# The first MLP product of the first layer by seven products of half blocks for eight, its operands in large tiles

## The chip, the cores and the metric

The kernel runs on one core of one Trainium2 chip. The metric is the device time of one execution in microseconds; the time of the kernel before is the median of three runs. The engines are PE (TensorE, the matmuls), DVE (VectorE), ACT (ScalarE), POOL (GpSimd) and SP (SyncE, which here issues the transfers). Each takes its instructions strictly in the order in which they stand in its program.

## The reference, cut to what matters

A trunk of two layers on 512 latent tokens and 256 context tokens of width 1024. Each layer has an attention part and a squared-ReLU MLP of hidden width 4096; the second layer runs its MLP on the latent tokens alone.

```python
def sq_relu_mlp(h, w1, w2):
    return jnp.square(jax.nn.relu(h @ w1)) @ w2
...
        x = x + mod_x[5] * sq_relu_mlp(modulate(rmsnorm(x, norm2_g[l]), mod_x[3], mod_x[4]),
                                       w_mlp_in[l], w_mlp_out[l])
        if not last:
            ctx = ctx + mod_c[5] * sq_relu_mlp(modulate(rmsnorm(ctx, norm2_g[l]), mod_c[3], mod_c[4]),
                                               w_mlp_in[l], w_mlp_out[l])
```

## The kernel before, in words

**Precision.** Every fp32 operand of a product is split into a high part (a cast) and a low part (what the cast left over), and a product is three matmuls: high by high, low by high, high by low. A weight comes by one transfer into a tile `raw`; ACT makes `wh` (L457), DVE makes `wl` (L458).

**The first product** of the first layer (`mlp1_chunks`): the 768 tokens are two halves of 384, the features of w_mlp_in are 32 chunks of 128, and the inner width 1024 is eight blocks of 128. For each chunk and half, 8 x 3 matmuls of 384 columns (L1083 to L1085) add up in one PSUM tile `psd` or `pss`: 48 a chunk, 96 for two. ACT takes the relu out of PSUM (L1090) and squares it to the high part `uh` (L1091); POOL squares it again in full precision (L1092) and DVE subtracts to get the low part `ul` (L1093). The tokens enter as `hT`, made by `norm_T`: PE transposes (L413), ACT applies the modulation (L420), DVE casts (L421), and DVE and POOL in turn make the low part (L423).

**The second product** (`mlp2`) is done by groups of four chunks: for each half of the output width, six PSUM tiles (one per 128 tokens) collect 12 matmuls of 512 columns each (L1117 to L1119). Then `resid` takes them out: DVE multiplies by the gate into `rtmp` (L719), POOL adds it to the tokens `xlat` or `xctx` (L720).

**The order.** There are eight groups. The code writes the first product of group g+1 ahead of the second product of group g. Between the chunks it calls `step`, which hands out pieces of the adaptive modulation of the next layer: a block of w_ada is loaded into `araw` (L276), and DVE adds it, scaled, to `acc` (L280, L282). A list scheduler then fixes one order for each engine before the program runs. Tiles come from pools by tag; a tag has so many buffers (`CAPS`), and a tile that finds none free makes its writer wait. The tag `re` with nine buffers serves `relu`, `acc`, `araw` and `arow`; `w4` with five serves `wh` and `wl`.

## Time and profile before

| | |
|---|---|
| time, median of three runs | 1664.24 us (1663.88 to 1664.32) |
| the profiled execution | 1664.7 us, its span 1662.8 us |
| PE busy | 1615.0 us, 97% of the span, 8994 instructions |
| DVE busy | 1010.4 us, 61% |
| ACT busy | 684.2 us, 41% |
| POOL busy | 610.5 us, 37% |
| mean granted clock of PE | 0.994 |

How to read it: the span goes from the first to the last instruction; the run's own time is 1.9 us more. The shares are averages over the whole span, in which the first layer's MLP lies between about 433 and 945 us. Matmuls overlap, so the busy time of one counts its latency. The views that follow below are the page, the waits of an engine, groups of instructions by shape, timelines and windows.

### The profile page before, as it was taken

The numbers are of one execution on the slowest core, as the hardware profiler recorded it, in microseconds if no ns is written. First come the engines' busy times: TensorE is split into PE (matmuls) and PEld (weight loads), VectorE is DVE, ScalarE is ACT, GpSimd is POOL, SyncE is SP. The second block draws the span as 40 slices with busy tenths as digits, with TensorE's granted clock in tenths as the row PEclk, the third lists the DMA queues.
The fourth block names the chain that finished last, engine by engine and source line by source line (L and its number), as shares of the span: only waits on it lengthen the run. The fifth ranks groups of instructions, "written<-read, shape, count | busy, mean of one in ns | idle before, by whom it ended". The sixth has DMA issues, their size and how long they took to land.

```text
span 1662.8 us, 24078 instructions
## 1 busy us (share of the span) xinstructions
PE 1615.0 (97%) x8994; PEld 1354.3 (81%) x8994; DVE 1010.4 (61%) x1995; ACT 684.2 (41%) x1342; POOL 610.5 (37%) x564
## 2 busy tenths in 40 slices
...
GB/s 319 179 167 112 134 35 26 67 65 13 33 184 134 120 115 114 115 102 125 90 106 116 236 51 74 62 60 39 42 82 15 66 98 91 102 101 97 93 106 72
DMA packets 156422, 164.47 MB, mean 99 GB/s; under 512 B 8960, under 2 KB 111368, under 8 KB 156304
## 3 DMA queue, kind: packets, MB, share of 16 engines
...
q14 instruction: 47, 0.39, 0.1%
...
## 4 chain that ended last, share of the span: by engine, by line
PE 89%; DVE 6%; DMA 2%; ACT 1%; issue 1%; POOL 0%; SPq 0%; POOLq 0%; DVEq 0%; ACTq 0%
PE psd L1083 9%; PE psd L1084 9%; PE psd L1085 9%; PE psv L669 5%; PE pss L611 5%; PE pst L660 5%; PE pss L1117 3%; PE pss L1118 3%; PE pss L1119 3%; PE psd L474 3%; PE psd L475 3%; PE psd L476 3%; PE pst L1119 2%; PE pst L1118 2%; PE psv L1118 2%; PE psv L1119 2%
## 5 line engine op out<-in xcount | busy, mean ns | idle before, releaser
L720 POOL TENSOR_TENSOR xlat<-xlat,rtmp 128x512 f32<-128x512 f32 x159 | 234.3, 1497 | 267.7 <-DVE rtmp L719 264.5
L458 DVE TENSOR_TENSOR wl<-raw,wh 128x1024 fp32r<-128x1024 f32 (+1 forms) x168 | 219.1, 1305 | 184.0 <-issue 72.2
L457 ACT CAST wh<-raw 128x1024 fp32r<-128x1024 f32 (+1 forms) x168 | 174.8, 1041 | 301.1 <-PE pst L1119 175.4
L1083 PE MATMUL psd<-hT,wh 128*128 128x384 f32 (+2 forms) x752 | 264.8, 353 | 3.9 <-DVE hT L421 3.9
L1084 PE MATMUL psd<-hT,wl 128*128 128x384 f32 (+2 forms) x752 | 264.2, 351 | 2.5 <-DVE wl L458 2.5
L1085 PE MATMUL psd<-hT,wh 128*128 128x384 f32 (+2 forms) x752 | 265.2, 353 | 0.1
L635 POOL TENSOR_TENSOR prob<-prob,sm 128x512 f32<-128x512 f32 (+3 forms) x110 | 126.9, 1161 | 256.3 <-DVE sm L628 175.8
L1092 POOL TENSOR_TENSOR relu<-relu 128x384 f32<-128x384 f32 (+1 forms) x96 | 97.6, 1018 | 314.1 <-ACT uh L1091 299.6
L1090 ACT ACTIVATE relu<-psd 128x384 f32<-128x384 f32 (+1 forms) x93 | 49.1, 528 | 279.4 <-PE psd L1085 276.4
L627 ACT ACTIVATE prob<-prob,m 128x513 f32<-128x513 f32 (+6 forms) x160 | 121.2, 758 | 94.3 <-DVE m L622 69.2
L1083 PEld LDWEIGHTS psd<-hT,wh 128*128 128x128 f32 x752 | 141.4, 188 | 15.7 <-DVE hT L421 4.4
L1093 DVE TENSOR_TENSOR ul<-relu,uh 128x384 fp32r<-128x384 f32 (+1 forms) x96 | 59.2, 617 | 152.7 <-POOL relu L1092 152.7
L1084 PEld LDWEIGHTS psd<-hT,wl 128*128 128x128 f32 x752 | 141.4, 188 | 12.8 <-DVE wl L458 3.2
L1085 PEld LDWEIGHTS psd<-hT,wh 128*128 128x128 f32 x752 | 141.3, 188 | 9.7 <-DVE hT L423 0.3
L282 DVE SCALAR_TENSOR_TENSOR acc<-araw,consts,acc 128x512 f32<-128x512 f32 x140 | 116.9, 860 | 15.0 <-DMA araw<-in_w_ada_dram 14.0
L660 PEld LDWEIGHTS pst<-consts,prob 128*128 128x128 f32 x688 | 77.8, 141 | 48.3 <-issue 37.5
L660 PE MATMUL pst<-consts,prob 128*128 128x128 f32 x688 | 114.2, 282 | 2.4 <-POOL prob L635 1.3
L476 PE MATMUL psd<-hT,wl 128*128 128x384 f32 (+1 forms) x280 | 97.1, 347 | 1.1 <-DVE wl L458 1.1
L474 PE MATMUL psd<-hT,wh 128*128 128x384 f32 (+1 forms) x280 | 97.8, 349 | 0.2 <-DVE rtmp L719 0.2
L475 PE MATMUL psd<-hT,wh 128*128 128x384 f32 (+1 forms) x280 | 97.1, 347 | 0.0
L664 ACT COPY pT<-pst 128x512 f32<-128x512 f32 x124 | 70.9, 585 | 62.8 <-PE pst L660 62.6
L1118 PE MATMUL pss<-wl,uh 128*128 128x512 f32 x224 | 87.4, 390 | 0.0
...
## 6 DMA issues: line engine op xcount, KB each, us to landing
...
araw<-in_w_ada_dram SPq DMA_DIRECT2D x112, 256.0 KB, 4.7
...
raw<-in_w_ada_dram SPq DMA_DIRECT2D x32, 256.0 KB, 5.7
...
raw<-in_w_out_dram SPq DMA_DIRECT2D x16, 256.0 KB, 3.7
```

The lines of the kernel that those rows point to most:

```text
L457: A.copy(hi, raw)
L458: V.tensor_tensor(lo, raw, bc(hi), ALU.subtract)
L474: T.matmul(ps[:, :n], wh[:, k, :], hh[k][:, s0:s0 + n], start=(k == 0), stop=False)
L475: T.matmul(ps[:, :n], wh[:, k, :], hl[k][:, s0:s0 + n], start=False, stop=False)
L476: T.matmul(ps[:, :n], wl[:, k, :], hh[k][:, s0:s0 + n], start=False, stop=(k == KC - 1))
L635: G.tensor_tensor(p_[:, :w_], p_[:, :w_], sm.to_broadcast([P, w_]), ALU.mult)
L660: T.transpose(pt[:, r * P:(r + 1) * P], pts[r][:, pos[r][kb]:pos[r][kb] + P], ident)
L720: (V if fast and (RLAST if fast == "end" and t == 3 else RFAST)[dh] == "V" else G).tensor_tensor(xt[t][:, cs], xt[t][:, cs], tmp, ALU.add)
L1083: T.matmul(o_, wh[:, k, :], hh[k][:, sl], start=(k == 0), stop=False)
L1084: T.matmul(o_, wl[:, k, :], hh[k][:, sl], start=False, stop=False)
L1085: T.matmul(o_, wh[:, k, :], hl[k][:, sl], start=False, stop=(k == KC - 1))
L1118: T.matmul(a_, uh[:, ts_], wl[:, c % 2, :], start=False, stop=False)
```

## The change

In the first layer alone, two chunks of features (256), the two halves of the inner width and the two halves of the tokens form a product of 2 x 2 blocks. It is now made by seven products of sums of blocks instead of eight products of blocks: 7 x 12 = 84 matmuls for two chunks.

- **Tokens:** `norm_seven` takes the place of `norm_T`. It makes the four blocks of tokens and their sums (L506 and L508 on DVE, L510 and L513 on POOL) and splits each of seven operands into high (L493 on DVE, L495 on ACT) and low (L496), four pieces of 384 each, into tiles `hseven`.
- **Weights:** `pair_left` loads the two chunks by two transfers and makes the sums in place by four operations on POOL (L1186 to L1189). Each of seven operands of 512 is split as it comes up: cast on ACT (L1180), low part on DVE (L1181).
- **Products:** `mlp1_pair` runs them in the order 1, 2, 6, 5, 7, 3, 4 (L1208 to L1210); some collect in the PSUM tile of an earlier one. Three times a pair ACT copies an intermediate out of PSUM (L1214), three times DVE adds it to another (L1225). Relu (L1222, L1226), square (L1227), full square on POOL (L1228) and low part (L1229) follow for each of the four blocks.
- **Order:** the code writes pair 1 of group g, then pair 0 of group g+1, then the second product of group g. Pair 0 and pair 1 of group 0 alternate.
- **Tiles:** high and low parts now share large tiles (`hT`, `kk`, `ot`, `xn`, `acc`, `upair`); the gates lie in the tile of constants; the rope and mask tables are loaded again in each layer. `re` has five buffers instead of nine (`acc` has one of its own), `w4` four instead of five, which now hold high and low part together. The last group's second-product weights lie in `hseven` tiles.

Lines moved: what was L457, L458 is L525, L526; L719, L720 are L786, L787; L280, L282 are L289, L291; L1117 to L1119 are L1286 to L1288.

```diff
-CAPS = {"tm": 4, "rt": 4, "pr": 8, "r0": 16, "re": 9, "raw": 4, "w4": 5, "pT": 4, "xn": 12,
-        "h1": 16, "h2": 16, "pg": 18, "cr": 1, "ct": 8, "kr": 5, "vc": 2, "kc": 8,
-        "up": 4, "u": 16, "wf": 16, "of": 8, "fg": 2, "ga": 4}
-PAD = ("pr", "tm", "xn", "pg", "up")
+CAPS = {"tm": 4, "rt": 4, "pr": 8, "r0": 16, "re": 5, "raw": 4, "w4": 4, "pT": 4, "xn": 6,
+        "h1": 8, "h2": 8, "pg": 18, "cr": 1, "ct": 8, "kr": 5, "vc": 2, "kc": 8,
+        "rA": 1, "kk": 6, "ot": 8, "ac": 1, "hs": 7, "uu": 3, "up": 4, "u": 12, "wf": 16, "of": 8, "fg": 2, "ga": 4}
+PAD = ("pr", "tm", "pg", "up")
...
-    ("re", "relu acc araw arow"),
+    ("re", "relu araw arow"),
...
+    ("ac", "acc"),
+    ("hs", "hseven"),
+    ("uu", "upair tb"),
+    ("kk", "kk"),
+    ("ot", "ot"),
...
-            acc = [[prob(512, name="acc") for _ in range(2)] for _ in range(nw)]
+            acc = view(prob(2048, name="acc"), [4, 512])
+            acc = [[acc[:, 2 * w + h_] for h_ in range(2)] for w in range(nw)]
...
+    def norm_seven(groups, l):
+        xns = [norm_xn(g) for g in groups]
+        cols = mod_cols(l, 2)
+        n = P * len(groups[0])
+        ops = {m: [None] * 4 for m in (1, 2, 3, 4, 5, 6, 7)}
+        flip = [0]
+        big = {}
+        def feat(k, gi, tf):
+            g, xn = groups[gi], xns[gi]
+            pt = ps_t()
+            for i in range(len(g)):
+                T.transpose(pt[:, i * P:(i + 1) * P],
+                            xn[i][k // 4][:, (k % 4) * P:(k % 4 + 1) * P], ident)
+            nx = P * sum(1 for t in g if t < 4)
+            for w, (c0, c1) in enumerate(((0, nx), (nx, n))):
+                if c1 > c0:
+                    a_, s_ = cols(k, w)
+                    A.activation(tf[:, c0:c1], pt[:, c0:c1], AF.Identity, bias=s_, scale=a_)
+            return tf
+        def split(m, j, src):
+            if ops[m][0] is None:
+                big[m] = page(8 * n, F32R, "hseven")
+            o_ = big[m][:, 2 * n * j:2 * n * j + 2 * n]
+            flip[0] ^= 1
+            if flip[0]:
+                V.tensor_copy(o_[:, :n], src)
+            else:
+                A.copy(o_[:, :n], src)
+            (G if flip[0] else V).tensor_tensor(o_[:, n:2 * n], src, bc(o_[:, :n]), ALU.subtract)
+            ops[m][j] = (o_[:, :n], o_[:, n:2 * n])
+        left, right = [[t_[:, 2 * n * j:2 * n * (j + 1)] for j in range(4)]
+                       for t_ in (page(8 * n, name="tb"), page(8 * n, name="tb"))]
+        for r, m in ((0, 1), (1, 2)):
+            for j in range(4):
+                split(m, j, feat(4 * r + j, 0, left[j][:, r * n:(r + 1) * n]))
+        for j in range(4):
+            b11, b21 = left[j][:, :n], left[j][:, n:]
+            b12, b22 = [feat(4 * r + j, 1, right[j][:, r * n:(r + 1) * n]) for r in range(2)]
+            V.tensor_tensor(b11, b12, b11, ALU.subtract)
+            split(5, j, b11)
+            V.tensor_tensor(b11, b22, b11, ALU.subtract)
+            split(6, j, b11)
+            G.tensor_tensor(b12, b22, b12, ALU.subtract)
+            split(7, j, b12)
+            split(3, j, b22)
+            G.tensor_tensor(b21, b21, b11, ALU.subtract)
+            split(4, j, b21)
+        return ops
...
+            hop = norm_seven(groups, l)
...
+        def pair_left(g, q):
+            f0 = (F0[g] + 2 * q) * P
+            r1, r2 = raw_tile([4, 256]), raw_tile([4, 256])
+            for i, r_ in enumerate((r1, r2)):
+                nc.sync.dma_start(r_, w_mlp_in[l, i * 512:(i + 1) * 512, f0:f0 + 256].rearrange("(k p) f -> p k f", p=P))
+            a11, a21, a12, a22 = r1[:, :, 0:P], r1[:, :, P:256], r2[:, :, 0:P], r2[:, :, P:256]
+            def split(src):
+                o_ = w_tile([8, P], "wh")
+                A.copy(o_[:, 0:4], src)
+                V.tensor_tensor(o_[:, 4:8], src, bc(o_[:, 0:4]), ALU.subtract)
+                return o_[:, 0:4], o_[:, 4:8]
+            e_ = view(prob(512, name="relu"), [4, P])
+            yield split(a11)
+            yield split(a12)
+            G.tensor_tensor(e_, a21, a22, ALU.add)
+            G.tensor_tensor(a21, a11, a21, ALU.subtract)
+            G.tensor_tensor(a11, e_, a11, ALU.subtract)
+            G.tensor_tensor(a12, a12, a11, ALU.subtract)
+            yield split(a11)
+            yield split(e_)
+            yield split(a21)
+            yield split(a12)
+            yield split(a22)
+        def mlp1_pair(g, q, new):
+            n = ntok // 2
+            left = pair_left(g, q)
+            u4 = page(4 * ntok, F32R, "upair")
+            u4 = [u4[:, i * ntok:(i + 1) * ntok] for i in range(4)]
+            u = us[g, 2 * q], us[g, 2 * q + 1] = (u4[0], u4[1]), (u4[2], u4[3])
+            def product(m, ps, first):
+                wh, wl = next(left)
+                for j in range(4):
+                    bh, bl = hop[m][j]
+                    more = dict(skip_group_check=True)
+                    T.matmul(ps[:, :n], wh[:, j, :], bh, start=(first and j == 0), stop=False, **more)
+                    T.matmul(ps[:, :n], wl[:, j, :], bh, start=False, stop=False, **more)
+                    T.matmul(ps[:, :n], wh[:, j, :], bl, start=False, stop=(j == 3), **more)
+            def out(ps):
+                t_ = prob(n, name="relu")
+                A.copy(t_, ps[:, :n])
+                return t_
+            def done(c, h, src, ps=None):
+                uh, ul = u[c]
+                sl = slice(h * n, (h + 1) * n)
+                if ps is None:
+                    r_ = prob(n, name="relu")
+                    A.activation(r_, src[:, :n], AF.Relu)
+                else:
+                    r_ = src
+                    V.tensor_tensor(r_, r_, ps[:, :n], ALU.add)
+                    A.activation(r_, r_, AF.Relu)
+                A.activation(uh[:, sl], r_, AF.Square)
+                G.tensor_tensor(r_, r_, r_, ALU.mult)
+                V.tensor_tensor(ul[:, sl], r_, bc(uh[:, sl]), ALU.subtract)
+            x_ = new()
+            product(1, x_, True)
+            p1 = out(x_)
+            y_ = new()
+            product(2, y_, True)
+            done(0, 0, p1, y_)
+            yield
+            product(6, x_, False)
+            u2 = out(x_)
+            y_ = new()
+            product(5, y_, True)
+            p5 = out(y_)
+            product(7, x_, False)
+            done(1, 1, p5, x_)
+            yield
+            product(3, y_, False)
+            done(0, 1, u2, y_)
+            product(4, x_, False)
+            done(1, 0, x_)
+            yield
+        def mlp1_by_pairs(g, q):
+            n = 2 if g < 2 else 1
+            if g == 0:
+                prs = [mlp1_pair(g, i, new) for i, new in ((0, ps_d), (1, ps_s))]
+                for pr_ in prs:
+                    next(pr_)
+                for pr_ in prs:
+                    for _ in pr_:
+                        step(n + 1)
+                return
+            for _ in mlp1_pair(g, q, ps_d):
+                step(n + (1 if g < 2 else 0))
...
-        mlp1(0)
+        if last:
+            mlp1(0)
+        else:
+            mlp1_by_pairs(0, 0)
         for g in range(NG):
-            if g + 1 < NG:
+            if last and g + 1 < NG:
                 mlp1(g + 1)
+            if not last and g:
+                mlp1_by_pairs(g, 1)
+            if not last and g + 1 < NG:
+                mlp1_by_pairs(g + 1, 0)
```

Below are places in the engines' orders. Names are tiles with their numbers: `rtmp` the gated output, `relu` and `psd` as above, `raw` the loaded weights, `relu` on L1186 the sum of two of their blocks.

POOL before, from the end of the second product of a group to the first product of a later one:

```order
L720 TENSOR_TENSOR xlat_69<-xlat_69,rtmp_6527 128x512
L720 TENSOR_TENSOR xlat_69<-xlat_69,rtmp_6530 128x512
L720 TENSOR_TENSOR xctx_70<-xctx_70,rtmp_6533 128x512
L720 TENSOR_TENSOR xctx_70<-xctx_70,rtmp_6536 128x512
L1092 TENSOR_TENSOR relu_6605<-relu_6605 128x384
L1092 TENSOR_TENSOR relu_6610<-relu_6610 128x384
L1092 TENSOR_TENSOR relu_6681<-relu_6681 128x384
```

POOL after, at the like place, the second pair of a group (product 6 of this pair needs the result of L1188):

```order
L787 TENSOR_TENSOR xlat_69<-xlat_69,rtmp_6421 128x512
L787 TENSOR_TENSOR xlat_69<-xlat_69,rtmp_6424 128x512
L787 TENSOR_TENSOR xctx_70<-xctx_70,rtmp_6427 128x512
L787 TENSOR_TENSOR xctx_70<-xctx_70,rtmp_6430 128x512
L1186 TENSOR_TENSOR relu_6447<-raw_6443,raw_6444 128x512
L1187 TENSOR_TENSOR raw_6443<-raw_6443 128x4x128
L1228 TENSOR_TENSOR relu_6463<-relu_6463 128x384
L1188 TENSOR_TENSOR raw_6443<-relu_6447,raw_6443 128x4x128
L1189 TENSOR_TENSOR raw_6444<-raw_6444,raw_6443 128x4x128
```

The four operations on the weights stand behind the residual additions of the second product, where before the next work was the squaring of a finished block.

ACT before, around the end of a chunk:

```order
L457 CAST wh_6625<-raw_6623 128x1024
L457 CAST wh_6701<-raw_6699 128x1024
L1090 ACTIVATE relu_6605<-psd_6555 128x384
L1091 ACTIVATE uh_6553<-relu_6605 128x384
L1090 ACTIVATE relu_6610<-psd_6556 128x384
L457 CAST wh_6777<-raw_6775 128x1024
L1091 ACTIVATE uh_6553<-relu_6610 128x384
```

ACT after, from the end of one pair to the first half of the next (`wh_6650` is the operand of product 6, `relu_6619` the block that product 2 finishes):

```order
L1222 ACTIVATE relu_6588<-psd_6442 128x384
L1227 ACTIVATE upair_6441<-relu_6588 128x384
L1214 COPY relu_6619<-psd_6598 128x384
L1226 ACTIVATE relu_6619<-relu_6619 128x384
L1227 ACTIVATE upair_6597<-relu_6619 128x384
L1180 CAST wh_6650<-raw_6599 128x512
L1180 CAST wh_6668<-relu_6603 128x512
```

Casts of weights stood ahead of the relu of the chunk that ran; now the cast for product 6 stands behind the relu and the square of the same pair's first block.

DVE before, in the first groups of the MLP:

```order
L282 SCALAR_TENSOR_TENSOR acc_5242<-araw_5248,consts_66,acc_5242 128x512
L1093 TENSOR_TENSOR ul_5111<-relu_5225,uh_5110 128x384
L282 SCALAR_TENSOR_TENSOR acc_5240<-araw_5252,consts_66,acc_5240 128x512
L1093 TENSOR_TENSOR ul_5121<-relu_5230,uh_5120 128x384
L282 SCALAR_TENSOR_TENSOR acc_5242<-araw_5252,consts_66,acc_5242 128x512
L1093 TENSOR_TENSOR ul_5121<-relu_5235,uh_5120 128x384
L1093 TENSOR_TENSOR ul_5263<-relu_5314,uh_5262 128x384
L458 TENSOR_TENSOR wl_5419<-raw_5416,wh_5418 128x1024
```

DVE after, up to the weights of product 6 of the first pair of group 1 (`wh_5485`); x2 are two of one form:

```order
L291 SCALAR_TENSOR_TENSOR acc_5236<-araw_5412,consts_66,acc_5236 128x512 x2
L1229 TENSOR_TENSOR upair_5132<-relu_5407,upair_5132 128x384
L1225 TENSOR_TENSOR relu_5446<-relu_5446,psd_5448 128x384
L291 SCALAR_TENSOR_TENSOR acc_5236<-araw_5416,consts_66,acc_5236 128x512 x2
L291 SCALAR_TENSOR_TENSOR acc_5236<-araw_5420,consts_66,acc_5236 128x512 x2
L291 SCALAR_TENSOR_TENSOR acc_5236<-araw_5469,consts_66,acc_5236 128x512
L1229 TENSOR_TENSOR upair_5424<-relu_5446,upair_5424 128x384
L291 SCALAR_TENSOR_TENSOR acc_5236<-araw_5469,consts_66,acc_5236 128x512
L291 SCALAR_TENSOR_TENSOR acc_5236<-araw_5473,consts_66,acc_5236 128x512 x2
L291 SCALAR_TENSOR_TENSOR acc_5236<-araw_5477,consts_66,acc_5236 128x512 x2
L1181 TENSOR_TENSOR wh_5485<-raw_5426,wh_5485 128x512
L1181 TENSOR_TENSOR wh_5503<-relu_5430,wh_5503 128x512
```

Steps of the modulation stood between the splits before as well; now a run of them stands ahead of the split for product 6.

## Rows read from the trace of the kernel before

**Rows 1.** The page's part 1: busy us, share of the span, instructions.
```profile
PE 1615.0 (97%) x8994; PEld 1354.3 (81%) x8994; DVE 1010.4 (61%) x1995; ACT 684.2 (41%) x1342; POOL 610.5 (37%) x564
```

**Rows 2.** Waits of PE, whole span: us in total, times, longest.
```profile
PE psa L255 <- DMA raw<-in_w_ada_dram: 13.7, 6, 9.5
PE psd L1083 <- DVE hT L421: 3.9, 2, 3.5
```

**Rows 3.** Windows in the first MLP: length, then busy us of each engine (instructions).
```profile
630.00:730.00 100.00, 100.00 (x508) 89.52 (x507) 57.02 (x74) 22.61 (x35) 36.13 (x29) 1.00 0.35 110
```

**Rows 4.** Groups by shape, 433 to 945, PE: count, busy us, mean ns.
```profile
L1083 PE MATMUL psd<-hT,wh 128*128 128x384 f32 x496 | 166.6, 337 | 3.5 <-DVE hT L421 3.5
```

**Rows 5.** Timeline of PE, 668 to 682: start, duration; 18 and 32 rows.
```profile
671.11 0.39 PE L1117 MATMUL pss<-wh,uh 128*128 128x512 f32 x1
...
674.96 0.39 PE L1119 MATMUL pst<-wh,ul 128*128 128x512 f32 x1
...
676.51 0.33 PE L1085 MATMUL psd<-hT,wh 128*128 128x384 f32 x1
...
681.88 0.33 PE L1083 MATMUL psd<-hT,wh 128*128 128x384 f32 x1
```

**Rows 6.** Timeline of POOL, 655 to 690: start, duration, and the idle time before.
```profile
672.76 6.03 POOL L720 TENSOR_TENSOR xlat<-xlat,rtmp 128x512 f32<-128x512 f32 x4 [8.83 <-DVE rtmp L719]
678.76 2.55 POOL L720 TENSOR_TENSOR xctx<-xctx,rtmp 128x512 f32<-128x512 f32 x2
681.26 0.83 POOL L1092 TENSOR_TENSOR relu<-relu 128x384 f32<-128x384 f32 x1
686.09 1.26 POOL L1092 TENSOR_TENSOR relu<-relu 128x384 f32<-128x384 f32 x1 [4.00 <-ACT uh L1091]
```

**Rows 7.** Line L720, 433 to 945: count, ns minimum/median/maximum, first and last start.
```profile
L720 POOL TENSOR_TENSOR xlat<-xlat,rtmp x52: 1277/1302/2362, 522.5 to 930.6; 128x512 f32<-128x512 f32 x52
```

**Rows 8.** Groups by shape, 433 to 945, ACT.
```profile
L1091 ACT ACTIVATE uh<-relu 128x384 fp32r<-128x384 f32 x64 | 33.4, 526 | 1.3
L1090 ACT ACTIVATE relu<-psd 128x384 f32<-128x384 f32 x62 | 30.5, 493 | 177.6 <-PE psd L1085 174.6 <-DMA arow<-in_b_ada_dram 3.0
L1134 ACT CAST wfh<-raw 128x512 fp32r<-128x512 f32 x8 | 4.7, 620 | 6.3 <-DMA raw<-in_w_mlp_out_dram 6.3
```

**Rows 9.** Groups by shape, 433 to 945, DVE.
```profile
L282 DVE SCALAR_TENSOR_TENSOR acc<-araw,consts,acc 128x512 f32<-128x512 f32 x136 | 112.4, 852 | 15.0 <-DMA araw<-in_w_ada_dram 14.0
...
L1093 DVE TENSOR_TENSOR ul<-relu,uh 128x384 fp32r<-128x384 f32 x64 | 36.2, 567 | 84.2 <-POOL relu L1092 84.2
L719 DVE TENSOR_TENSOR rtmp<-pst,gates 128x512 f32<-128x512 f32 x26 | 17.8, 683 | 0.0
...
L280 DVE TENSOR_SCALAR acc<-araw,consts 128x512 f32<-128x512 f32 x20 | 12.5, 642 | 2.8 <-DMA araw<-in_w_ada_dram 2.8
...
L421 DVE CAST hT<-tf 128x384 fp32r<-128x384 f32 x16 | 7.8, 495 | 4.3 <-ACT tf L420 4.0
L1135 DVE TENSOR_TENSOR wfl<-raw,wfh 128x512 fp32r<-128x512 f32 x8 | 5.6, 724 | 2.0 <-ACT wfh L1134 2.0
L423 DVE TENSOR_TENSOR hT<-tf,hT 128x384 fp32r<-128x384 f32 x8 | 5.1, 643 | 0.2
```

**Rows 10.** Tile araw, 433 to 945: count, ns minimum/median/maximum.
```profile
L282 DVE SCALAR_TENSOR_TENSOR acc<-araw,consts,acc x136: 736/747/1833, 461.4 to 944.2; 128x512 f32<-128x512 f32 x136
```

**Rows 11.** The page's part 6: DMA issues, count, KB each, us to landing.
```profile
araw<-in_w_ada_dram SPq DMA_DIRECT2D x112, 256.0 KB, 4.7
```

**Rows 12.** Windows of 2 us: busy us of the engines, then PEclk, the granted clock.
```profile
432.00:434.00 2.00, 0.77 (x2) 0.77 (x3) 2.00 (x5) 1.11 (x4) 0.68 (x1) 0.67 0.22 55
434.00:436.00 2.00, 2.00 (x9) 1.90 (x9) 1.96 (x4) 0.92 (x3) 0.84 (x2) 0.50 1.05 323
436.00:438.00 2.00, 2.00 (x14) 1.97 (x13) 1.60 (x3) 0.29 (x1) 1.43 (x2) 0.98 0.11 40
758.00:760.00 2.00, 0.49 (x4) 0.17 (x2) 1.71 (x2) 1.53 (x3) 0.00 (x0) 1.00 0.00 0
```

55 lines of the change are left out of this document (36 added, 19 removed).

## The prediction

> **What bounds the kernel now.** Read first the shares of the engines: PE 97% of the span, DVE 61%, ACT 41%, POOL 37% [rows 1]. Then the waits of PE: beside 13.7 us at the start of the program there is near the change only one of some size, 3.9 us on the casts of the normed tokens, 3.5 of it in one piece [rows 2]. A stretch of 100 us inside the first layer's MLP has PE 100.00 busy while DVE is busy 57.02, ACT 22.61, POOL 36.13 [rows 3]. So in this stage the kernel runs at the pace of PE, and the others arrive early. What a matmul costs there must not be taken from its mean: a 128x384 product shows 337 ns [rows 4], but the starts of 32 in a row lie between 676.51 and 681.88, 31 gaps, 0.173 us each; the 512-wide ones of the last pass of mlp2 go from 671.11 to 674.96 in 17 gaps, 0.226 us each [rows 5]. The mean is the latency of one, of which the next hides half.
>
> **What the change saves.** 16 pairs of feature chunks need 84 matmuls instead of 96, so 192 fewer, at 0.173 us: **-33.3 us**, if PE stays fed. The Trainium skill (Perfetto Trace Analysis, Identifying the Most-Contended Engine) says that matmul busy time is a poor measure of PE because pipelined instructions mislead; the trace agrees, 337 ns against 173; by the mean the saving would be 64.7 us and the whole sum below 31 us lower.
>
> **What it adds, and where it lands.** Four things become late for PE, which takes the products of a pair in the order 1, 2, 6, 5, 7, 3, 4 with nothing between 2 and 6 in most pairs. Products 1 and 2 are 24 matmuls, 4.2 us; product 6 needs a weight sum that only exists after three additions on POOL, a cast on ACT and a subtraction on DVE.
>
> (a) *Second pairs of groups 1 to 6.* In POOL's order the additions (L1186 to L1188) stand behind the twelve residual additions of the mlp2 just ahead. Before, the end of such an mlp2 can be watched: the last matmul starts at 674.96, so ends E = 675.2, while POOL's residual additions run until 681.3, E+6.1 [rows 5, 6]; today behind them stands only a squaring for which nobody on PE is in a hurry. After: E+6.1, then two additions at 1.3 (the nearest row is the residual addition, 512 wide in POOL, 1.28 to 2.36, median 1.30), one squaring L1228 at 0.83 to 1.26, one more addition at 1.3 [rows 6, 7], then the cast of 512 at 0.62 on ACT [rows 8]: E+11.4. PE has worked until E+4.2. So 7.2 us of idle PE, six times: **+43 us**. Bounds: 5.5 us where the residual ends earlier and the squaring goes in between, 10 us where POOL's additions run at their longest: +33 to +60. In the last group 18 matmuls of mlp2 (18 x 0.226 = 4.1 us) stand between products 2 and 6: about **+4** there (0 to 6).
> The Trainium skill (GPSIMD Engine Reference, Engine selection) puts elementwise two-input work on VectorE, as twice as fast; here the row of POOL is 1.30 and that of DVE for the same width 0.68 [rows 7, 9], so the rule speaks against this placing, by 3 x 0.62 = 1.9 us for each such chain.
>
> (b) *First pairs of groups 2 to 7.* Two chains of the same length. On ACT the cast for product 6 stands behind relu and square of the block that product 2 finishes: DVE addition 0.6, relu 0.49, square 0.53, cast 0.62 [rows 8, 9] and the handing over between four engines, 2.2 to 3 us in which PE has nothing. On POOL the three additions stand behind the last squaring of the pair before: 0.49 + 0.53 + 1.0 + 3 x 1.3 + 0.62 = 6.5 us after that pair's end, against 4.2 us of work, 2.3 us and the handing over. I take 2.8 us: six times, **+17 us** (12 to 24).
>
> (c) *The opening: normed tokens and groups 0 and 1.* Before, DVE has 16 casts and 8 low parts of 384 tokens to make here; now half of 28 pairs of them, and eight of sixteen sums, and after them, in its order, the steps of the adaptive modulation (L289, L291) ahead of the weight splits. From the first cast to the split for product 6 of group 1's first pair DVE has 26 x 0.852 + 4 x 0.642 (modulation) + 14 x 0.495 (casts) + 14 x 0.643 (low parts) + 17 x 0.567 (sums and low parts of activations) + 15 x 0.724 (weight splits of 512, by the row of the same width) + 7 x 0.57 (sums out of PSUM, scaled from the 0.683 of 512) + some 3 for five others = 68 us [rows 9]. PE has before this point 192 matmuls of 384 and 48 transposes, 33.3 + 2.8 = 36 us (a 128x128 transpose taken as a third of a product). **+32 us.** Of these about 13 fall in the very opening: to the fourth operand of the first product 6 DVE has 28 us of the same rows, PE 13 and some. Lower bound 22: everything at the price that it has when POOL is still, the modulation steps at 0.747 instead of 0.852 [rows 10]. Upper bound 50: the buffers of the modulation's weight blocks, nine before and shared, are five after, now shared with more tiles of the activation, and a block takes 4.7 us to land [rows 11]; 15 blocks that wait a little more than 1 us each.
>
> (d) *The clock of PE.* In the trace, behind the stall of 3.5 us, the granted clock is 0.67 in 432-434 and 0.50 in 434-436, then 0.98 [rows 12]; 0.50 of 2.4 GHz is the lower level, 1.2 GHz. Half of the 2 us busy there and some 0.4 of the 0.77 us before it: about 1.4 us lost. A hole of 1.5 us (758-760) shows 1.00 [rows 12]. So I add 1.4 us for the large stalls, nine of them: **+13 us** (0 to 20, if it also falls in the short ones).
>
> Costed at nothing: the three copies out of PSUM per pair on ACT and the extra DVE sums, except where named, since ACT and DVE are idle for 77 and 43 of 100 us [rows 3]; if that cover is gone, at most 16 x (3 x 0.5) = 24 us, of which the range holds what the sum is short of its end. The larger tiles, the rope table read again and layer 1: the same matmuls in nearly the same order, 0 with 5 us to either side, since no row shows what four buffers for split weights instead of five do.
>
> **The sum**, against the profiled run's own 1664.7 us (span 1662.8; 0.5 above the median of three): 1664.7 - 33.3 + 43 + 4 + 17 + 32 + 13 = **1740 us**, 4.6% slower. All low ends give 1693, all high ends 1796 (the 5 us of layer 1 to either side among them).
>
> **Rivals.**
> *PE stays the bound.* If the additions and splits arrive before product 6 (POOL done with the residual sooner than before, or the pairs' weights loaded early enough to be summed ahead), only the opening is left: 1664.7 - 33.3 + 13 = 1644 us, faster. For it: POOL is busy only 36 of 100 us [rows 3]. Against it: POOL takes its work in the written order, and [rows 6] has the residual's end 6.1 us after E while PE needs the sum at E+4.2. It decides from the point where (a), (b), (d) and the rest of (c) come to less than 20 us together, 1.5 us a pair; none of them needs more than its own late end to be over that. The Trainium skill's rule that the most contended engine is the one to relieve (the same section) would come out here, since PE is at 97% [rows 1].
> *Only the short chain.* POOL's sums are hidden after all, but ACT's order stays: 13 pairs x 2.8 = 36, opening 32: 1664.7 - 33.3 + 36 + 32 = 1700 us. For: the ACT chain needs no POOL. Against: as above.
> *The five buffers.* The blocks of the modulation wait for buffers through groups 1 to 4 too, and with them DVE and the splits behind: 15 to 20 blocks more at 2 to 4 us, 40 to 60 us on top, about 1800 to 1830. For: of 15.0 us that DVE stands idle ahead of these steps, 14.0 already end with such a block [rows 9]. Against: DVE has 43 of 100 us spare [rows 3].
> That the change doesn't remove the matmuls is no rival: the count follows from the code.
>
> **How the numbers follow.** The forecast 0.72; the short chain 0.12; the five buffers 0.05; PE-bound 0.08; stalls that just eat the 33 us, 0.03. Range: 1690 to 1800 holds forecast and short chain, less some 0.04 at the edges. 0.2% (3.3 us) is about what a measurement of this kernel tells from no change. Faster by more: 0.08; within: 0.03; slower by more: 0.89.
>
> **What would show it.** In the changed kernel's waits of PE, L1208 behind DVE or ACT weights of 512 (L1180, L1181), some 80 to 100 us in all; PE's share down from 97% to about 91%; on the timeline of POOL, L1186 starting without a gap behind the L787 burst, and PE idle 7 us from E+4.2 in groups 1 to 6, 2 to 3 us in the first pairs; DVE at 9 of 10 or more through the first 70 us of the MLP, with L291 ahead of L1181; PEclk 0.5 behind each large hole. (a) is wrong if L1188 ends before E+4.2; (c) is wrong if DVE has holes there that end with anything but POOL or a block's landing; (d) is wrong if the clock stays at 1.00. The prediction is wrong as a whole if PE has no wait at L1208, or if the waits sum to under 33 us.

## The result, and the profile after

| | before | after |
|---|---|---|
| time, median of four runs each | 1664.06 us (1660.40 to 1664.32) | 1814.97 us (1813.16 to 1815.59) |
| ratio, 95% interval | | 1.09 (1.0884 to 1.0917) |
| span of the profiled execution | 1662.8 us | 1811.4 us |
| mean granted clock of PE | 0.994 | 0.948 |

The change makes the kernel 9% slower. The forecast had the sign and the places, but at 1740 us (1690 to 1800) it is 75 us too low, and the time lies outside the range.

The page of the kernel after: part 1, and of part 2 (40 slices of 45 us, in tenths) the rows of PE and of its granted clock.

```profile
PE 1638.8 (90%) x8802; PEld 1355.1 (75%) x8802; DVE 1167.7 (64%) x2137; ACT 744.4 (41%) x1484; POOL 740.6 (41%) x642
...
PE   6999999999468697898979799999999999999998
...
PEclk9999999999679798998989899999999999999999
```

Against [rows 1], the 192 matmuls are gone (8994 to 8802), yet PE is busy 24 us longer, and its share falls from 97% to 90%. Slices 11 to 24, the first layer's MLP, show why: PE is idle there, and its granted clock is lower, at which the same work keeps it busy longer.

Windows over this stage, from its first to its last product; columns: stretch, length, busy us (instructions) of PE, PEld, DVE, ACT, POOL, then PEclk, DMA share, GB/s. The kernel before:

```profile
433.00:980.00 547.00, 544.63 (x2778) 488.93 (x2779) 332.39 (x441) 146.50 (x244) 207.74 (x164) 1.00 0.38 121
```

The kernel after:

```profile
437.00:1123.00 686.00, 562.42 (x2577) 488.85 (x2578) 454.16 (x571) 207.76 (x386) 314.45 (x241) 0.89 0.30 95
```

The stage grows by 139 us, from 547 to 686. PE is idle for 123.6 us of it, where it was idle for 2.4; and in windows of 1 us, busy time multiplied by what the clock is short of 1.00 sums to 46.3 us, where it was 1.4. Ahead of the stage the kernel after is 4.3 us late, behind it 5.4 us longer. So the whole 148.6 us of the spans is: 33.3 saved, 121.2 more idle, 44.9 more lost to the clock, 9.7 outside the stage, and 6.1 that no row assigns. An estimate takes up most of these: the last matmul ahead of a stall is busy for its whole 0.33 us, where the next one would hide half of it, and the stage after has 31 stalls above 0.5 us, so 31 x 0.16 = 5.0 us.

Waits of PE in the stage after: us in total, times, longest.

```profile
PE psd L1208 <- ACT wh L1180: 80.8, 14, 13.5
PE psd L297 <- DVE acc L291: 10.2, 1, 10.2
PE pss L1208 <- ACT wh L1180: 8.6, 1, 8.6
PE psd L1210 <- DVE hseven L496: 5.9, 4, 1.7
PE psd L1209 <- DVE wh L1181: 5.0, 6, 3.8
```

Where [rows 2] had 3.9 us on the normed tokens, fifteen waits for split weights of a pair (L1180), nearly all of them of product 6, now take 89 us. By place:

| place | predicted us | measured idle us |
|---|---|---|
| opening, groups 0 and first pair of group 1 | 32 | 41.8 (and 1.9 just ahead of the stage) |
| second pairs of groups 1 to 6 | 43 | 42.7 (10.30, 6.89, 6.52, 6.44, 6.45, 6.06) |
| second pair of group 7 | 4 | none at product 6; 3.4 just ahead of it, at L1318 and L1320 |
| first pairs of groups 2 to 7 | 17 | 22.35 (1.78, 7.85, 3.78, 1.38, 3.78, 3.78) |
| L297, a matmul of the modulation, behind DVE's steps | not in the sum | 10.25 |
| clock | 13 | 44.9 |

**A second pair, group 3.** Timeline of the kernel after, all engines, rows left out between: start, duration, engine, operation, idle time before it and its releaser.

```profile
753.41 5.49 POOL L787 TENSOR_TENSOR xlat<-xlat,rtmp 128x512 f32<-128x512 f32 x4 [7.26 <-DVE rtmp L786]
...
758.74 0.33 PE L1210 MATMUL psd<-hseven,wh 128*128 128x384 f32 x1
...
758.86 2.51 POOL L787 TENSOR_TENSOR xctx<-xctx,rtmp 128x512 f32<-128x512 f32 x2
...
759.78 0.34 PE L1210 MATMUL psd<-hseven,wh 128*128 128x384 f32 x1
...
761.33 1.26 POOL L1186 TENSOR_TENSOR relu<-raw 128x512 f32<-128x512 f32 x1
762.67 1.26 POOL L1187 TENSOR_TENSOR raw<-raw 128x512 f32<-128x512 f32 x1
763.89 0.82 POOL L1228 TENSOR_TENSOR relu<-relu 128x384 f32<-128x384 f32 x1
764.67 1.26 POOL L1188 TENSOR_TENSOR raw<-relu,raw 128x512 f32<-128x512 f32 x1
...
765.97 0.62 ACT L1180 CAST wh<-raw 128x512 fp32r<-128x512 f32 x1 [4.07 <-POOL raw L1188]
...
766.64 1.21 PE L1208 MATMUL psd<-hseven,wh 128*128 128x384 f32 x2 [6.52 <-ACT wh L1180]
...
768.89 0.52 PE L1208 MATMUL psd<-hseven,wh 128*128 128x384 f32 x1
769.21 0.52 PE L1209 MATMUL psd<-hseven,wh 128*128 128x384 f32 x1
```

Read it upwards: PE waits for the cast, ACT has been idle for 4.07 us until L1188, and POOL is never idle from 753.41 on. The residual additions (as in [rows 6]), two sums, one squaring, one sum: the chain of the forecast, link by link. Ahead of the stall, from 758.74 to 759.78, matmuls start in six steps of 0.173 us, as in [rows 5]; behind it, in the last two rows, 0.32 apart.

Only the 10.30 us of group 1 are not this chain alone. There the sum is ready at 588.9, but the cast starts 3.4 us later, and the trace names a modulation step of DVE as its releaser:

```profile
587.28 1.59 POOL L1188 TENSOR_TENSOR raw<-relu,raw 128x512 f32<-128x512 f32 x1
...
591.48 0.74 DVE L291 SCALAR_TENSOR_TENSOR acc<-araw,consts,acc 128x512 f32<-128x512 f32 x1
592.29 0.62 ACT L1180 CAST wh<-raw 128x512 fp32r<-128x512 f32 x1 [7.86 <-DVE acc L291]
```

**The clock behind the same stall.** Windows of 1 us of the kernel after, columns as above.

```profile
759.00:760.00 1.00, 1.00 (x7) 0.80 (x5) 0.00 (x0) 0.00 (x0) 1.00 (x1) 1.00 0.99 315
...
766.00:767.00 1.00, 0.36 (x1) 0.28 (x1) 0.73 (x2) 1.00 (x2) 0.99 (x1) 0.50 0.00 0
...
769.00:770.00 1.00, 1.00 (x5) 1.00 (x4) 0.83 (x2) 0.00 (x0) 0.00 (x0) 0.50 0.06 16
770.00:771.00 1.00, 1.00 (x5) 1.00 (x4) 0.00 (x0) 0.00 (x0) 0.00 (x0) 0.51 0.00 0
771.00:772.00 1.00, 1.00 (x8) 1.00 (x7) 0.00 (x0) 0.38 (x2) 0.00 (x0) 1.00 0.00 0
```

Before the stall the clock is 1.00 of 2.4 GHz; at the restart it is 0.50, the lower level of 1.2 GHz, and it stays there for 4.4 us, of which PE is busy 4.1. These 4.1 us between 766 and 771 (0.84 and 0.92 in the two windows left out, at 0.50 as well) lose half: 2.1 us. Behind the 3.78 us stall of the next first pair it is 0.50 to 0.53 from 788 to 791, too, and from 457 to 487, in the opening, it is 0.50 in the mean of 30 us with PE busy 16.87 of them. Behind each of the ten stalls above 6 us, 2.0 to 3.6 us are lost within 8 us. Short stalls go either way: behind the 1.38 us of group 5, with 0.72 us idle just before, 1.7 us are lost, behind the 1.78 us of group 2 none.

**The opening.** Windows of the kernel after: the whole of it, and the piece that holds its longest stall.

```profile
437.00:532.00 95.00, 53.23 (x230) 45.98 (x230) 83.70 (x103) 38.93 (x83) 55.34 (x44) 0.71 0.21 66
...
517.00:532.00 15.00, 1.49 (x7) 0.93 (x5) 15.00 (x17) 2.75 (x6) 8.64 (x6) 0.66 0.00 0
```

DVE is busy 83.70 us where the forecast had 68. Its groups there by shape (busy us, mean ns):

```profile
L291 DVE SCALAR_TENSOR_TENSOR acc<-araw,consts,acc 128x512 f32<-128x512 f32 x26 | 26.3, 1061 | 0.0
L496 DVE TENSOR_TENSOR hseven<-tb,hseven 128x384 fp32r<-128x384 f32 x14 | 12.4, 894 | 2.5 <-ACT hseven L495 2.5
L1181 DVE TENSOR_TENSOR wh<-raw,wh 128x512 fp32r<-128x512 f32 x13 | 11.9, 929 | 4.0 <-ACT wh L1180 4.0
L493 DVE CAST hseven<-tb 128x384 fp32r<-128x384 f32 x14 | 9.2, 667 | 0.0
...
L508 DVE TENSOR_TENSOR tb<-tb 128x384 f32<-128x384 f32 x4 | 4.8, 1218 | 0.0
...
L1225 DVE TENSOR_TENSOR relu<-relu,psd 128x384 f32<-128x384 f32 x4 | 2.2, 544 | 1.5 <-PE psd L1210 1.5
```

The counts are those of the forecast (with the smaller groups left out, 15 splits of weights and 7 sums out of PSUM), and every price shown but one is higher: 1061 ns for 852 of [rows 9], 894 for 643, 929 for 724, 667 for 495, 1218 where 567 was taken. Only L1225, which reads one of its two inputs from PSUM, costs 0.54 us, about the 0.57 expected. That points at POOL, busy 55.34 of the same 95 us; experiments below test it.

### The profile page after: what moved, and what is told of

The parts are those of the page before. It is cut to its first block, busy times and chain, and to the rows that moved or that the text cites. A ratio compares the mean times of both kernels' runs of the same rounds, so it can differ in the third digit from the quotient of the medians.

```text
span 1811.4 us, 24131 instructions
## 1 busy us (share of the span) xinstructions
PE 1638.8 (90%) x8802; PEld 1355.1 (75%) x8802; DVE 1167.7 (64%) x2137; ACT 744.4 (41%) x1484; POOL 740.6 (41%) x642
## 4 chain that ended last, share of the span: by engine, by line
PE 72%; DVE 11%; issue 6%; POOL 5%; ACT 2%; DMA 1%; POOLq 0%; DVEq 0%; ACTq 0%
PE psv L736 5%; PE pst L727 5%; PE pss L678 4%; PE psd L1159 3%; PE psd L1160 3%; PE psd L1158 3%; PE psd L1209 3%; PE psd L1208 3%; PE pss L1286 3%; PE pss L1287 3%; PE pss L1288 3%; PE psd L542 3%; PE psd L1210 3%; PE psd L544 3%; PE psd L543 3%
## 5 line engine op out<-in xcount | busy, mean ns | idle before, releaser
L787 POOL TENSOR_TENSOR xlat<-xlat,rtmp 128x512 f32<-128x512 f32 x159 | 246.0, 1572 | 334.4 <-DVE rtmp L786 329.1
L1208 PE MATMUL psd<-hseven,wh 128*128 128x384 f32 x420 | 159.4, 384 | 88.9 <-ACT wh L1180 80.8
L526 DVE TENSOR_TENSOR wl<-raw,wh 128x1024 fp32r<-128x1024 f32 (+1 forms) x136 | 195.2, 1442 | 58.0 <-ACT wh L525 57.9
L525 ACT CAST wh<-raw 128x1024 fp32r<-128x1024 f32 (+1 forms) x136 | 140.1, 1036 | 80.3 <-PE pst L1288 35.2
L694 ACT ACTIVATE prob<-prob,m 128x513 f32<-128x513 f32 (+6 forms) x160 | 121.0, 756 | 122.4 <-DVE m L689 74.3
L1208 PEld LDWEIGHTS psd<-hseven,wh 128*128 128x128 f32 x420 | 90.2, 215 | 100.3 <-ACT wh L1180 89.2
L1209 PE MATMUL psd<-hseven,wh 128*128 128x384 f32 x420 | 155.7, 371 | 5.1 <-DVE wh L1181 5.0
L1210 PE MATMUL psd<-hseven,wh 128*128 128x384 f32 x420 | 154.2, 368 | 6.6 <-DVE hseven L496 5.9
L1228 POOL TENSOR_TENSOR relu<-relu 128x384 f32<-128x384 f32 x64 | 64.7, 1010 | 220.9 <-ACT upair L1227 197.7
L291 DVE SCALAR_TENSOR_TENSOR acc<-araw,consts,acc 128x512 f32<-128x512 f32 x140 | 133.5, 983 | 2.8 <-DMA araw<-in_w_ada_dram 2.4
L1181 DVE TENSOR_TENSOR wh<-raw,wh 128x512 fp32r<-128x512 f32 x96 | 86.3, 917 | 56.7 <-ACT wh L1180 56.7
L727 PEld LDWEIGHTS pst<-consts,prob 128*128 128x128 f32 x688 | 77.8, 142 | 50.3 <-issue 37.9
L786 DVE TENSOR_TENSOR rtmp<-pss,consts 128x512 f32<-128x512 f32 x66 | 44.8, 688 | 108.0 <-PE pss L1288 101.2
L1180 ACT CAST wh<-raw 128x512 fp32r<-128x512 f32 x96 | 57.2, 618 | 121.9 <-PE pst L1288 43.8
L1158 PE MATMUL psd<-hT,wh 128*128 128x512 f32 (+1 forms) x256 | 98.2, 384 | 1.6 <-ACT wh L525 0.9
L1159 PE MATMUL psd<-hT,wl 128*128 128x512 f32 (+1 forms) x256 | 98.1, 383 | 1.7 <-DVE wl L526 1.7
L1160 PE MATMUL psd<-hT,wh 128*128 128x512 f32 (+1 forms) x256 | 98.4, 385 | 0.3 <-POOL hT L436 0.3
```

The source lines that it names most:

```text
L526: V.tensor_tensor(lo, raw, bc(hi), ALU.subtract)
L727: T.transpose(pt[:, r * P:(r + 1) * P], pts[r][:, pos[r][kb]:pos[r][kb] + P], ident)
L787: (V if fast and (RLAST if fast == "end" and t == 3 else RFAST)[dh] == "V" else G).tensor_tensor(xt[t][:, cs], xt[t][:, cs], tmp, ALU.add)
L1158: T.matmul(o_, wh[:, k, :], hh[k][:, sl], start=(k == 0), stop=False)
L1159: T.matmul(o_, wl[:, k, :], hh[k][:, sl], start=False, stop=False)
L1160: T.matmul(o_, wh[:, k, :], hl[k][:, sl], start=False, stop=(k == KC - 1))
```

## The experiments

The theory after the result: PE waits because the weight sums, and the steps that DVE must do first, come late in engines that work in order; each such wait also costs clock behind it. Against it stand the five buffers (the rival of the forecast) and DVE's number of instructions as the cause of the opening. In the table, idle and loss are those of PE in the stage, reckoned as above; the ratio is to the kernel before, run on the same chip at the same time. The kernel before took 1663 to 1667 us in these rounds, so rows that lie a few us apart are compared by the ratio.

| kernel | time us | ratio (95%) | idle us | clock loss us |
|---|---|---|---|---|
| after | 1814.97 | 1.09 (1.0884 to 1.0917) | 123.6 | 46.3 |
| e1, sums on DVE | 1769.83 | 1.0633 (1.0602 to 1.0664) | 87.4 | 37.7 |
| e2, nine buffers | 1806.18 | 1.0851 (1.0820 to 1.0883) | 120.1 | 46.8 |
| e4, PE kept busy | 1799.91 | 1.0814 (1.0782 to 1.0845) | 77.5 | 30.4 |
| e5, modulation out of the pairs | 1784.84 | 1.0723 (1.0692 to 1.0754) | 102.2 | 39.6 |
| e6, before with four `w4` | 1683.22 | 1.0099 (1.0070 to 1.0128) | 8.1 | 1.6 |
| e7, token casts on ACT | 1812.34 | 1.0874 (1.0842 to 1.0905) | 120.5 | 50.3 |
| e8, all of it ahead | 1688.54 | 1.0131 (1.0102 to 1.0160) | 36.7 | 10.7 |
| e9, e8 with sums on DVE | 1692.10 | 1.0152 (1.0123 to 1.0182) | 34.7 | 18.3 |
| e10, tokens off POOL | 1811.11 | 1.0889 (1.0858 to 1.0921) | 122.4 | 45.0 |
| e11, e8 and e10 | 1682.86 | 1.0118 (1.0089 to 1.0147) | 27.1 | 15.4 |
| e12, e11 with group 0's sums on DVE | 1680.23 | 1.0102 (1.0066 to 1.0139) | 27.1 | 11.0 |

**e1: the four weight sums on DVE.**

```diff
-            G.tensor_tensor(e_, a21, a22, ALU.add)
+            V.tensor_tensor(e_, a21, a22, ALU.add)
```
(and the three below it)

> The four additions on the weights (L1186 to L1189) on DVE instead of POOL, nothing else. Theory (POOL's order sets the wait of the second pairs): the sums no longer stand behind the residual additions, so in groups 2 to 6 the wait ahead of product 6 of the second pair falls from 6.1-6.9 us to under 3 us; with the loss at the low clock about 20 to 25 us less, 1790 to 1800 us, because DVE gets 64 operations more (some 44 us of work), which holds the opening where it is or makes it worse. Rival (the order on ACT, the cast behind relu and square, sets it): the waits stay at 6 us and the time at 1815 or above.

45 us come back, more than expected. The stalls of the second pairs of groups 3 to 5 fall from 6.5 to 1.7 us for the cast and another 1.7 for the low part; the first pairs of groups 4, 6 and 7 from 3.78 to 2.7. So POOL's place in the chain makes 3 of the 6.5 us of such a stall; the rest stays with the cast and the low part. Of the 36.2 us less idle, 19 are at the second pairs, 8 at the first pairs, 5 at L297 and 4 in the opening. At the last three the sums had run beside DVE's steps, and e1 doesn't separate their place from what the two engines cost each other; e8 and e9, with the sums on POOL and on DVE, do. The forecast weighed the rule of the Trainium skill (GPSIMD Engine Reference, Engine selection) that two-input work belongs on VectorE at 1.9 us a chain, the difference of the durations; what counted more was the queue that the sums stood in, 3 us a stall and the clock behind it.

**e2: the shared buffers back to nine.**

```diff
-        "re": 5,
+        "re": 9,
```

> Nine buffers instead of five for the tag that holds the modulation's weight blocks and the activation's tiles, nothing else. Rival of the prediction (the five buffers cost 40 to 60 us): 1755 to 1775 us. Theory (DVE's and POOL's orders): DVE stands idle only 2.4 us for such a block in the changed kernel, so at most 5 us either way, 1810 to 1820 us.

9 us, not 40 to 60, a little more than the 5 expected: in the profiled executions 2.7 in the stage, where the 13.51 us stall becomes 6.64 and 4.09, and 4.9 behind it. The rival of the five buffers falls.

**e4: matmuls that nobody uses, between products 2 and 6.** 32 in the second pairs, 16 in the first pairs, in groups 1 to 7 except (1,0) and (7,1); 288 more in all, their results dropped.

```diff
+            w2_ = last_w[0]
+            y_ = new()
+            for i in range(FILL(g, q)):
+                T.matmul(y_[:, :n], w2_[:, i % 4, :], hop[2][i % 4][0], start=True, stop=True, skip_group_check=True)
             product(6, x_, False)
             u2 = out(x_)
-            y_ = new()
```
(`w2_` is the high part of product 2's weights)

> Between products 2 and 6, PE gets matmuls of which nothing is kept (their result is overwritten by product 5): 32 in the second pairs of groups 1 to 6, 16 in the first pairs of groups 2 to 7; 288 more matmuls, 50 us of PE's work put into time in which it was idle. Theory (the granted clock falls because PE stands idle, and costs 46 us in this stage, some 2 us a stall): the clock stays at 1.00 behind the filled stalls, and the time falls by 10 to 25 us although PE has more to do, 1790 to 1805 us. Rival (the clock falls for another reason, or the filling only pushes product 6 back): 1815 to 1835 us.

288 matmuls more and 15 us less. PE's stall ahead of product 6 in the second pairs of groups 3 to 5 is 1.0 us, and in the stage 15.9 us of the clock loss are gone. In three first pairs a wait of 2.2 to 4.4 us stands ahead of the fillers instead, for the tile that they write, which DVE still has to read. This separates the clock from the wait: it is a cost of its own, laid on top of the stalls.

**e5: the modulation's steps out of the pairs.** They go ahead of and into the second product; of the pairs from group 1 on only (1,0) keeps four. One row of the modulation is made a second time on PE in this kernel, 64 small matmuls.

```diff
-            for _ in mlp1_pair(g, q, ps_d):
-                step(n + (1 if g < 2 else 0))
+            for i, _ in enumerate(mlp1_pair(g, q, ps_d)):
+                step(4 if (g, q, i) == (1, 0, 0) else 0)
...
-                step(STEPS)
+                step(STEPS if last else 4)
...
+            if not last:
+                step(4)
             mlp2(g)
```

> The steps of the modulation (L289, L291) are handed out between the first products and the second product of a group, not between the products of a pair; their number stays. Theory (in the first pairs DVE's order, steps of 1.7 us each ahead of the sum L1225, sets the wait): in groups 3, 4, 6 and 7 the wait ahead of product 6 of the first pair falls from 3.8-7.9 us to 2.5 us or less, the 10.3 us wait on an accumulator in group 2 goes, that of group 1's second pair falls from 10.3 to 6.5 us; the second pairs of groups 2 to 6 keep their 6 us. About 20 us of idle PE and 6 us at the low clock less: 1785 to 1795 us. Rival (POOL's three additions behind the last squaring set it): the first pairs keep 3.8 us and the time is 1805 or above.

30 us back; in the profiled executions 20.3 in the stage and 9.0 behind it. Every first pair from group 2 on now stalls for 2.68 us; the wait at L297 is gone, the 10.30 of group 1 is 5.56, and the 13.51 of the opening is 9.25. (Before that cast the trace of either kernel names a modulation step L291 of DVE as the releaser; in the kernel after POOL's sum had ended 3 us earlier.) Against what was expected, group 2's second pair stalls longer, 9.07 us for 6.89. Behind two of the six stalls of 2.68 us 1.7 us are lost to the clock, behind the other four none. So the chain on ACT that the forecast priced at 2.8 us is 2.68, and what the first pairs cost beyond it came from the steps. Group 3 shows how. Timeline of the kernel after, all engines:

```profile
698.71 3.01 DVE L291 SCALAR_TENSOR_TENSOR acc<-araw,consts,acc 128x512 f32<-128x512 f32 x2
...
702.91 1.46 POOL L1188 TENSOR_TENSOR raw<-relu,raw 128x512 f32<-128x512 f32 x1
703.17 3.41 DVE L291 SCALAR_TENSOR_TENSOR acc<-araw,consts,acc 128x512 f32<-128x512 f32 x2
...
706.51 0.54 DVE L1225 TENSOR_TENSOR relu<-relu,psd 128x384 f32<-128x384 f32 x1
707.08 0.52 ACT L1226 ACTIVATE relu<-relu 128x384 f32<-128x384 f32 x1 [7.78 <-DVE relu L1225]
707.64 0.52 ACT L1227 ACTIVATE upair<-relu 128x384 fp32r<-128x384 f32 x1
708.07 0.60 ACT L1180 CAST wh<-raw 128x512 fp32r<-128x512 f32 x1
...
708.72 1.21 PE L1208 MATMUL psd<-hseven,wh 128*128 128x384 f32 x2 [7.85 <-ACT wh L1180]
```

The sum is ready at 704.4. But ACT's cast stands behind relu and square, these behind DVE's L1225, and that behind four modulation steps at 1.5 to 1.7 us each, twice the 0.747 of [rows 10], while POOL works beside them.

**e6: the kernel before, with four `w4` buffers instead of five.**

```diff
-        "raw": 4, "w4": 5,
+        "raw": 4, "w4": 4,
```

> The kernel before with four buffers instead of five for split weights (tag w4), nothing else: no product by seven, none of the large tiles. In the changed kernel some 4 us are lost ahead of the MLP and 5 us behind it. Theory (the smaller buffers outside of the first layer's MLP cost these 10 us): 1670 to 1680 us. Rival (the large tiles or the tables loaded again cost them): 1662 to 1667 us.

1% slower by this alone, 16.4 us against the kernel before of its own round, somewhat more than expected. Against the profile of the kernel before, whose round was some 2 us faster, it is 5.1 us ahead of the stage, 6.9 in it, 7.6 behind it. Outside the stage the split weights are of the same size in both kernels, so the 4.3 us that the kernel after loses ahead of the stage have a sufficient cause. For the 5.4 behind it that is not shown: with four `w4` buffers as well, that part is in e2 only 0.4 us longer than in the kernel before, and in e5 and e8 it is 3.7 and 2.0 us shorter. What makes these 5.4 us stays open.

**e7: all 28 casts of the token operands on ACT.**

```diff
-            if flip[0]:
-                V.tensor_copy(o_[:, :n], src)
-            else:
-                A.copy(o_[:, :n], src)
+            A.copy(o_[:, :n], src)
```

> The changed kernel with all 28 casts of the token operands on ACT instead of half of them on DVE. Theory (DVE's queue sets the opening): 14 casts of 0.67 us, 9 us, leave DVE; of the 44 us that PE is idle up to product 6 of group 1's first pair 5 to 10 us go, and 2 to 4 us of low clock with them: 1800 to 1810 us. Rival (ACT or the chain of one operand's steps sets it): 1812 to 1820 us.

A miss: 14 operations off DVE bring 2.6 us; 3.2 us less idle stand against 4.0 more lost to the clock. By the intervals the time itself is the same as that of the kernel after. The number of DVE's instructions alone does not set the opening.

**e8: everything ahead.** A second pair's products 1 and 2 and its sums are issued between the two halves of the second product ahead of it, its product 6 after the second half; a first pair's weights and sums are made in the pair before; the cast for product 6 stands ahead of the relu, the modulation's steps in the second products; token casts as in e7. The sums stay on POOL. The modulation row of e5 is made on PE alone.

```diff
+            w6 = next(left)
             done(0, 0, p1, y_)
-            yield
-            product(6, x_, False)
+            product(6, x_, False, w6)
...
             for dh in range(2):
+                if dh and mid is not None:
+                    next(mid)
...
+                if i == 0 and g + 2 < NG:
+                    ready = prep(g + 2, 0)
```

> What the theory says should help, together, with the additions still on POOL: products 1 and 2 of the second pair of a group, its weight additions too, stand ahead of the last half of the second product of the group before (72 matmuls, 16.3 us, between products 2 and 6); the first pair's weights and additions are made ready during the pair before; the modulation's steps stand only around the second product, four in the opening; the last modulation row of this layer is made on PE (64 small matmuls) instead of by 32 DVE steps; the token casts are all on ACT. Theory (each wait is a matter of order, none of the work as such): outside of the opening no wait of more than 1 us ahead of product 6, the clock at 1.00 there; the opening keeps 15 to 25 us: 1670 to 1695 us. Rival (DVE, ACT and POOL have too much work for seven products, wherever it stands): waits of 2 to 6 us come back at other products, 1720 us or above.

126 us come back with the sums on the same engine. The version changes several things at once and gives PE a modulation row that DVE made, but DVE is busy as long as before in the stage (452.65 us, 454.16 in the kernel after), so there isn't less work for it; what changed is when it stands ready. Waits of PE behind the opening, 560 to 1005:

```profile
PE psd L1211 <- DVE wh L1178: 7.0, 6, 2.7
PE pss L1295 <- DVE wl L523: 2.3, 2, 1.2
PE psd L1210 <- DVE relu L1227: 0.5, 1, 0.5
```

And POOL there, the like place of a second pair:

```profile
681.95 3.19 POOL L784 TENSOR_TENSOR xctx<-xctx,rtmp 128x512 f32<-128x512 f32 x2
685.08 2.29 POOL L1183 TENSOR_TENSOR relu<-raw 128x512 f32<-128x512 f32 x1
...
689.36 1.62 POOL L1185 TENSOR_TENSOR raw<-relu,raw 128x512 f32<-128x512 f32 x1
```

The sums are slower than in the kernel after (1.6 to 2.3 us) and still stand behind the residual, but PE doesn't wait for them: half a second product lies between them and product 6. Not all was as expected: the two longest waits left, 2.7 and 2.4 us, are at product 3 of two second pairs, for a low part of DVE. With **e9**, the same with the sums on DVE, the engine no longer matters (the intervals of the two ratios overlap):

```diff
-            G.tensor_tensor(e_, a21, a22, ALU.add)
+            V.tensor_tensor(e_, a21, a22, ALU.add)
```

> As the run before, with the weight additions on DVE instead of POOL. Theory: once they stand ahead, the engine that makes them doesn't matter outside of the opening, within 5 us of the run before; in the opening DVE has 12 additions more (8 us), so up to 8 us slower. Rival (POOL's work lengthens DVE's by contention): 5 to 15 us faster than the run before.

**e10: in the kernel after, the two-input work of the tokens off POOL.** 22 operations more on DVE.

```diff
-            (G if flip[0] else V).tensor_tensor(o_[:, n:2 * n], src, bc(o_[:, :n]), ALU.subtract)
+            V.tensor_tensor(o_[:, n:2 * n], src, bc(o_[:, :n]), ALU.subtract)
...
-            G.tensor_tensor(b12, b22, b12, ALU.subtract)
+            V.tensor_tensor(b12, b22, b12, ALU.subtract)
```
(and the same for `b21`)

> The changed kernel with all of the token operands' work of two inputs on DVE: the 14 low parts and 8 sums that POOL had in the opening. Theory (DVE and POOL hold each other up: in the opening an operation of two inputs takes 0.55 us on DVE while POOL is still and 1.34 us while POOL works, POOL's 1.31 us each): what POOL did costs DVE 22 x 0.55 = 12 us and gives back 0.7 us on some 30 others, 20 us: the opening up to group 1's first pair gets 5 to 15 us shorter, 1800 to 1812 us. Rival (DVE's queue is simply its count of instructions): 10 to 15 us longer, 1825 us or above.

Windows and groups of DVE over the same 95 us of e10:

```profile
437.00:532.00 95.00, 53.47 (x235) 45.59 (x236) 80.81 (x130) 41.20 (x87) 32.72 (x22) 0.76 0.22 69
```

```profile
L496 DVE TENSOR_TENSOR hseven<-tb,hseven 128x384 fp32r<-128x384 f32 x28 | 15.5, 594 | 0.1
...
L493 DVE CAST hseven<-tb 128x384 fp32r<-128x384 f32 x14 | 4.8, 353 | 0.6 <-ACT tb L484 0.6
...
L508 DVE TENSOR_TENSOR tb<-tb 128x384 f32<-128x384 f32 x4 | 2.2, 554 | 0.0
```

DVE does 130 instructions instead of 103 in 80.81 us instead of 83.70. The low parts fall from 894 to 594 ns, the casts from 667 to 353, the sums from 1218 to 554. The whole time is the same by the intervals, where the rival had 10 to 15 us more. So the work on POOL had cost DVE as much as doing it itself.

**e11 and e12: e8 with that edit, then with group 0's weight sums on DVE too.**

```diff
+            E = V if g == 0 else G
-            G.tensor_tensor(e_, a21, a22, ALU.add)
+            E.tensor_tensor(e_, a21, a22, ALU.add)
```

> The version with products and additions ahead (the additions on the weights on POOL), and in the opening all work of two inputs on the token operands on DVE. Theory (contention): the opening's 31 us of idle PE become 18 to 26 us, and some of its 10 us at the low clock go: 1674 to 1684 us. Rival (count of DVE's instructions): 1695 us or above.

> As the run before, with the additions on the weights of group 0's two pairs on DVE as well (eight of 0.69 us), so that POOL has only the squarings in the opening. Theory (contention): 0 to 6 us faster than the run before. Rival (count of DVE's instructions): 4 to 6 us slower than it.

Both within what was expected, and both clear of the rival of e11 (1695 us or above); but the intervals of e8, e11 and e12 overlap, so no gain of one over the other is shown. e12 has the lowest time and is still 1.0% slower than the kernel before. Its stage, windows as above:

```profile
437.00:995.00 558.00, 530.93 (x2641) 463.07 (x2642) 443.09 (x565) 208.66 (x402) 293.21 (x212) 0.97 0.36 118
```

Of its 27.1 us idle 19.9, and all of the 11.0 us of clock loss, lie ahead of 594. Idle and loss, less what the kernel before has of them, take back 34.3 of the 33.3 us saved, most of it in the opening. Of the 10 us more that the stage has, 3.9 are the 64 matmuls of the modulation row on PE (0.061 us apart) and some 3, by the estimate made above, the ends of matmuls ahead of 17 stalls; the rest stays open.

## Why the prediction was right or wrong

The term that takes the time out of the range is the clock, (d): with 44.9 in place of 13 and all else as forecast the sum would be 1772 us, and without its excess the measured time would be 1783, both inside. The other misses are smaller.

- **The saving** is as reckoned: 192 matmuls fewer, and in the undisturbed stretches their starts stay 0.173 us apart.
- **(a) second pairs**: the mechanism is right, the chain of L787, L1186, L1187, L1228, L1188 and L1180 as written down; e1 and e8 show it by taking it away. That the sum agrees to 0.3 us (42.7 measured, 43 predicted) is in part luck: groups 2 to 6 stall for 6.5 us each and not 7.2, and 3.4 of the 10.30 us of group 1 are a wait behind DVE's steps, which the term did not have. In the last group PE stands idle for 3.4 us where 4 were taken, but for another operand: the matmuls of the second product between products 2 and 6 wait for activations (2.08 us at L1318 behind ACT's L1227, 1.29 at L1320 behind DVE's L1229), not product 6 for its weights.
- **(b) first pairs**: the chain on ACT is right (2.68 us by e5, 2.8 taken). The step that failed here is what stands ahead of L1225 on DVE: the modulation's steps, which the forecast counted in the opening alone. With them the first pairs wait 22.35 us instead of 17, and PE waits another 10.25 us at L297, for a row of the modulation, which the sum did not have at all.
- **(c) the opening**: right in place, 41.8 for 32. The count of DVE's instructions held; their prices did not. They were taken from rows of the kernel before, where POOL is busy 36 us of 100 [rows 3]; here it is 58. Term by term the measured means add 22 us to the 68, of which 15.7 show in the busy time (83.70), since instructions overlap. e7 had not told that (fewer instructions, no gain), e10 did (more instructions, no loss). The upper bound of 50 was drawn from the blocks' landing, not from this; by e2 that is worth 3 us in the stage.
- **(d) the clock**: the step that failed most, 13 predicted, 44.9 measured, above even the 20 of its upper end. The 1.4 us were read from one stall of 3.5 us whose work came back within 2 us [rows 12]; behind the stall shown the low level lasts through 4.4 us, 2.1 us lost. And the hole of 1.5 us without a loss was taken as a licence for all short ones, while each stall of 3.78 us is followed by 1.7 to 2.6 us lost, shorter ones sometimes by 1.7 and sometimes by none, and the opening's chain of stalls loses 12.9 us in 95. From 627 on, where eleven pairs stall, 59.4 us idle are followed by 26.0 lost. e4 confirms that it goes with the stalls.
- **Tiles and layer 1 at nothing**: wrong by 9.7 us. The `w4` buffers, named as the unknown, were given 5 us to either side; e6 has 12.7 us (some 2 less by its own round) for four instead of five outside this stage, which covers the 4.3 ahead of it. The 5.4 behind it are gone in e5 and e8 and nearly so in e2, all with the same four, so their cause stays open.
- **The rivals**: PE as the bound falls by 124 us of idle; the short chain alone by (a); the five buffers by e2, though 1815 lies inside the range it named: the right time for a wrong reason.
- Together: 31.9 for the clock, 9.8 for the opening, 10.25 for L297, 9.7 outside the stage, 5.4 for the first pairs, less 0.9 for the second ones, make 66 of the 73 us that the span is above the sum. The remaining 7 are small waits, 0.7 more than before, and the 6.1 that no row assigns.
